# A two-layer diffusion backbone on one core: the second layer's context scores and query preparation put elsewhere in a unit's order

## The chip, the cores and the metric

One Trainium2 chip, of which the program uses one core. The metric is device time in microseconds (us) of one execution. The engines are called PE (TensorE matmul), DVE (VectorE), ACT (ScalarE), POOL (GpSimd) and SP (SyncE, which issues the DMAs).

## The reference

The program runs two layers over 1024 latent tokens with 256 context tokens in front. The first layer (windowed attention and gated mixing) is not touched. The second is multi-head latent attention with 16 heads; what matters of it is this:

```python
def odd_layer(hl, hc, w_in, q_norm, w_qb, kv_norm, w_kvb, w_out, row, col, need_ctx):
    q_a, kv_a, k_pe, gate = jnp.split(hl @ w_in, ODD_SPLITS, axis=-1)
    q = mla_queries(q_a, q_norm, w_qb, row, col)
    k, v = mla_keys_values(kv_a, k_pe, kv_norm, w_kvb, row, col)
    ...
    kc, vc = mla_keys_values(kv_ac, k_pec, kv_norm, w_kvb, None, None)
    o = block_attention(q, jnp.concatenate([k, kc], axis=1), jnp.concatenate([v, vc], axis=1))
    y = (o * jax.nn.silu(gate)) @ w_out
```

So every latent query is scored against 1280 keys (1024 latent, 256 context), goes through a softmax, is multiplied by the values, gated, and projected.

## The kernel before, in words

The attention of the second layer (`layer1_attention`) goes over 64 **units** n. A unit is one head (e = 0 or 1 of the pair hp) and 256 queries (block qg of four); an even unit takes head 0 of a pair and the odd unit after it head 1 with the same 256 queries. The 256 queries stand in two halves j of 128. Eight pairs, four blocks, two heads make 64 units. A unit's work is an exact softmax: scores, maximum, exponential, transposes of the probabilities, products with the values. Products that need more than one pass are split into a high and a low fp32r part.

PSUM has 8 banks: `s0` and `s1` (two each: the 128x1024 scores of the two halves with the latent keys), `sx` (one: both halves' 128x256 scores with the context keys), `tm` (two, taken in turn: transposes and side projections) and `acc` (one: in columns 0 to 255 the products with the values, in columns 256 to 511 the inverse sums).

The order of everything in a unit is written out by hand in `ORDER1` (line 43), and the instructions of PE, ACT, DVE and POOL stand in just that order. The letters, for unit n:

- `S0` to `S3`: latent scores (lines 1228, 1229), one for each 512 columns; `S0 S1` fill `s0`, `S2 S3` fill `s1`. `S4`: the six products of the context's scores into `sx` (lines 1228, 1229, 1231). `K`: the rotary part, four products of 32 rows into `s0` and `s1` (line 1240), which end the latent scores.
- `X0 X1 X2`: maxima on DVE of `s0`, `s1`, `sx` (lines 1251, 1249). `P0 P1`: the two maxima joined (line 1255). `E0 E1`: exponential on ACT of `s0`, `s1`; `E2 E3`: of the two halves of `sx` (line 1266). `E0` must come before the next unit's `S0`, since `s0` is there once.
- `T0` to `T4`: transposes of the probabilities of unit n-1 into `tm`, four of 128x128 each (line 1276), and their copy out: `T0` and `T4` by DVE (line 1285), `T1 T2 T3` by ACT (line 1283). `T0 T1` are half j = 0, `T2 T3` half j = 1, `T4` the context's keys.
- `A0`: half of the products with the values for the pair of units before (line 1294). In an even unit they are keys 0 to 4 of units n-2 and n-1, so they read what `T0` to `T3` of this very unit deliver; in an odd unit keys 5 to 9 of units n-3 and n-2.
- `I`, `U` (odd units): inverse sums, spread by POOL, transposed into `acc` (line 1309). `C` (even units): `gated`, two DVE operations that read `acc` (lines 1318, 1320) and leave it free.
- `D`, `L`: one step each of the side work that prepares the next pair's keys (`prep_pair`) or values (`prep_v`): `D` a projection into `tm`, `L` its copy out. The table `PAIR, VALUES` says in which unit. Keys: ACT copies the high part (line 1153), DVE subtracts the low part (line 1155). Values: ACT copies them (line 1134).
- `B`, `R` (even units): the two steps of `prep_q` for the next 256 queries. `B` loads the rotary part (`pe`, SP, line 1167) and makes six products into a bank (lines 99 to 101). `R`: ACT copies the high part (line 1176), DVE subtracts the low part (line 1178), POOL makes `qc` and `qb` (lines 91, 95).

The table `PAIR, VALUES` gives these kinds of units by their place s in a run of 16: an even unit has a projection of values at s = 6, 10, 12, 14 (in the first three runs), of 512 keys at s = 4, and none otherwise; an odd unit has 512 keys at s = 3, 9, 11, 256 keys at s = 5, 13, and values or none otherwise. Of the 31 even units with a `B` (n = 0 to 60) 12 have values, 4 have 512 keys and 15 have none.

Of the kernel before, what the change touches and what calls it, by code (L numbers as in the profile page):

```python
# [17 lines left out]
D = 1024  # L18
# [21 lines left out]

PAIR, VALUES = (2, 3, 4, 5, 8, 9, 11, 13), (1, 6, 7, 10, 12, 14)
WQ = 'VGG'
ORDER1 = 'S0 S1 T0 T1 I C S2 D S3 K L X0 T2 S4 T3 X2 P0 E0 B X1 P1 E2 R A0 E1 T4 E3 U'.split()
AVS = ((0, 5),), ((5, 10),)
TURNS = 'VAAAV'
KPE = {3: [0], 5: [1]}
# [6 lines left out]
class Kernel:  # L53
# [1103 lines left out]
                self.hi("G", ring[e][0][64:128, c], ring[e][0][0:64, c].bitcast(F32))  # L1157
            yield

    def prep_q(self, hp, qg):  # L1160

        nc = self.nc
        pool = self.qpool[qg % len(self.qpool)]
        cols = slice(qg * self.QG, (qg + 1) * self.QG)
        pe = self.t(self.c1, [P, 2, self.QG], F32, "pe", bufs=1)
        for r in range(0, P, 32):
            nc.sync.dma_start(pe[r:r + 32], self.pe_d[64 * hp:64 * hp + 64, cols].rearrange("(e p) c -> p e c", e=2))
        tp = self.bank()
        w = self.wq[hp]
        for k in range(2):  # L1170
            self.mm3(tp[:, 0:self.QG], *w[k], self.qnh[:, k, cols], self.qnl[:, k, cols], k == 0, k == 1)
        yield
        qa, qb, qc = (self.t(pool, [P, 2, self.QG], F32R, tag, bufs=1) for tag in ("qa", "qb", "qc"))
        src = [tp[64 * e:64 * e + 64, 0:self.QG] for e in range(2)]
        for e in range(2):
            nc.scalar.copy(qa[0:64, e], src[e])  # L1176
        for e in range(2):
            nc.vector.tensor_tensor(qa[64:128, e], src[e], qa[0:64, e].bitcast(F32), op=ALU.subtract)  # L1178
        self.hi("G", qc, pe)
        self.lo("G", qb[96:128], pe[96:128], qc[96:128])  # L1180
        self.hi("G", qb[64:96], pe[64:96])
        self.hi("G", qb[0:64], qa[0:64].bitcast(F32))
        self.pq[(hp, qg)] = [(qa[:, e], qb[:, e], qc[:, e]) for e in range(2)]
        yield

    def layer1_attention(self):
# [24 lines left out]
        banks, peaks, probs, pts, accs, totals, spread = {}, {}, {}, {}, {}, {}, {}  # L1211
# [57 lines left out]
        def turn(n, a):  # L1269
# [14 lines left out]
            else:  # L1284
                nc.vector.tensor_copy(dst, src)  # L1285

        def av(m, k0, k1):
            hp, qg, _ = units[2 * m]
            if k0 == 0:
                accs[m] = self.psum("acc")  # L1290
            for kt in range(k0, k1):
                for e in range(2):
                    vc = ((2 * hp + e) % 4) * 64
                    mm(accs[m][64 * e:64 * e + 64, 0:QG], lhsT=self.v4[hp // 2][:, kt, vc:vc + 64],  # L1294
                       rhs=pts[2 * m + e][:, kt], start=kt == 0, stop=kt == NT - 1)
# [30 lines left out]
        def plan_q(n):  # L1326
            hp, g = n // 8, n % 8 // 2 + 1
            hp, g = (hp + 1, 0) if g == 4 else (hp, g)
            return [self.prep_q(hp, g)] if n % 2 == 0 and hp < 8 else []

        def plan(n):
            s, hp = n % 16, n // 8
# [13 lines left out]
        with self.tc.manual_schedule(engines={E.PE, E.Activation, E.DVE, E.Pool}):  # L1346
            for n in range(N + 3):
                odd = n % 2
                for op in ORDER1:
                    o, a = op[0], int(op[1:] or 0)  # L1350
# [11 lines left out]
                    elif o in "AIU":  # L1362

                        m = (n - 2 - odd) // 2
                        if 0 <= m < N // 2:
                            if o == "A":
                                av(m, *AVS[odd][a])
                            elif odd and o == "I":
                                inverses(m)
                            elif odd:  # L1370
                                inverses_out(m)
                                if n == N + 1:
                                    next(first)
                    elif o == "C":
                        for k in list(accs):
                            if k <= (n - 4) / 2:
                                gated(k)
                    elif o == "B":
                        qs = plan_q(n) if n < N else []
                        for p in qs:  # L1380
                            next(p, None)
                    elif o == "R":
                        for p in qs:
                            next(p, None)
                    elif o == "D":
                        preps = plan(n) if n < N else []
                        for p in preps:
                            next(p, None)
                    elif o == "L":
                        for p in preps:  # L1390
                            next(p, None)
# [214 lines left out]
```

## Time and profile before

| what | value |
|---|---|
| median of 3 runs | 1489.81 us (1490.66, 1489.81, 1485.21) |
| the profiled execution | 1485.86 us, span 1484.1 us |
| busy over the span | PE 1419.7 us (96%), DVE 884.6 (60%), ACT 726.6 (49%), POOL 479.2 (32%) |
| granted TensorE clock over the span | 0.995 |
| the 64 units | about 803 to 1395 us of the span |

The profile was taken of one execution, whose own time is 1485.86 us, 1.76 us more than its span. A PE row of the timeline gives the start and the length of a product, but products overlap: the length (0.28 us for 256 columns) runs until the result is out, while the next one starts after about 0.12 us. What a product costs PE is therefore the distance from its start to the next start, and a wait shows as a distance that is longer than usual.

### The profile page before, as it was taken

How to read it: one execution, taken by the hardware profiler on the slowest of the kernel's cores; microseconds unless marked ns; L12 is line 12 of the kernel's file. 1: busy time of each engine (PE TensorE's matmuls, PEld its weight loads, DVE VectorE, ACT ScalarE, POOL GpSimd, SP SyncE). 2: the span in 40 equal slices, each digit the busy share in tenths (PEclk: the TensorE clock that was granted, in tenths of full speed). 3: DMA queues.
4: the chain of work that ended last, by engine and by line, in shares of the span. 5: the costliest groups of instructions: out<-in, count | busy, mean ns of one | idle time of the engine just before them, and what ended most of it. 6: DMA issues, size and time to landing. Idle time of an engine off the chain costs nothing.

```text
span 1484.1 us, 23403 instructions
## 1 busy us (share of the span) xinstructions
PE 1419.7 (96%) x8849; PEld 1092.8 (74%) x8849; DVE 884.6 (60%) x1692; ACT 726.6 (49%) x1532; POOL 479.2 (32%) x495
## 2 busy tenths in 40 slices
PE   5999999999999699999997999999999999999997
PEld 3766899787666478879886677777777777776786
DVE  5582124346667887543663666776667667776354
ACT  4422310145656644433423666666666666677221
POOL 4343223223556642332183222132213221234100
PEclk9999999999999999999999999999999999999999
DMA  8557501222214446412132110111011111222241
GB/s 332 228 217 272 151 29 30 79 88 79 69 51 157 152 138 192 153 60 79 40 116 94 31 35 29 33 35 35 29 33 34 35 35 45 73 61 90 72 162 72
DMA packets 91465, 138.96 MB, mean 94 GB/s; under 512 B 9088, under 2 KB 67656, under 8 KB 88280
## 3 DMA queue, kind: packets, MB, share of 16 engines
q1 hardware_dynamic: 91208, 137.21, 27.8%
q8 instruction: 69, 1.13, 0.3%
q14 instruction: 44, 0.36, 0.1%
q10 hardware_dynamic: 144, 0.26, 0.0%
HBM read 105.88 MB, written 31.56 MB: 93 GB/s over the span
## 4 chain that ended last, share of the span: by engine, by line
PE 74%; DVE 8%; ACT 6%; issue 5%; DMA 4%; POOL 2%; SPq 0%; POOLq 0%; DVEq 0%; ACTq 0%
PE tm L1276 9%; PE acc L1294 7%; PE s L99 7%; PE s L100 7%; PE s L101 7%; PE b L99 5%; PE b L100 4%; PE b L101 4%; PE s L1228 4%; PE s L1229 3%; PE acc L773 2%; PE tm L99 2%; ACT prob L1266 1%; PE s L1240 1%; DVE kl L1155 1%
## 5 line engine op out<-in xcount | busy, mean ns | idle before, releaser
L1276 PE MATMUL tm<-ident,prob 128*128 128x128 f32 x1280 | 190.6, 279 | 5.1 <-DVE qa L1178 3.4
L1276 PEld LDWEIGHTS tm<-ident,prob 128*128 128x128 f32 x1280 | 141.9, 140 | 59.3 <-issue 22.8
L1283 ACT COPY pt<-tm 128x512 f32<-128x512 f32 x192 | 112.9, 588 | 137.2 <-PE tm L1276 135.6
L1251 DVE TENSOR_REDUCE peak<-s 128x1 f32<-128x1024 f32 x128 | 156.0, 1219 | 29.8 <-PE s L1240 29.1
L1266 ACT ACTIVATE prob<-s,peak 128x1024 f32<-128x1024 f32 x128 | 142.7, 1115 | 37.0 <-DVE peak L1255 34.7
L1294 PE MATMUL acc<-pt,v 128*64 128x256 f32 x1280 | 152.9, 384 | 0.1
L95 POOL TENSOR_TENSOR w_lo<-raw,w_hi 128x512 fp32r<-128x512 f32 (+1 forms) x60 | 74.3, 1251 | 172.2 <-ACT w_hi L87 85.6
L1285 DVE COPY pt<-tm 128x512 f32<-128x512 f32 x128 | 88.4, 690 | 67.2 <-PE tm L1276 65.8
L1294 PEld LDWEIGHTS acc<-pt,v 128*64 128x64 f32 x1280 | 86.4, 136 | 47.3 <-issue 6.1
L1228 PE MATMUL s<-kh,qa 128*128 128x512 f32 x256 | 112.2, 438 | 7.7 <-ACT prob L1266 6.1
L1229 PE MATMUL s<-kl,qb 128*128 128x512 f32 x256 | 101.1, 395 | 0.0
L91 POOL CAST qb<-qa 64x512 fp32r<-64x512 f32 x32 | 19.5, 611 | 190.4 <-ACT qa L1176 190.4
L99 PE MATMUL b<-h,yh 128*128 128x512 f32 x160 | 63.9, 399 | 3.9 <-ACT yh L87 2.9
L99 PE MATMUL s<-h,w_hi 128*128 128x512 f32 x160 | 63.9, 412 | 2.2 <-ACT qk L379 2.2
L100 PE MATMUL s<-h,w_hi 128*128 128x512 f32 x160 | 63.7, 398 | 0.3 <-DVE rs_v L124 0.3
L100 PE MATMUL b<-h,yh 128*128 128x512 f32 x160 | 63.3, 396 | 0.0
L101 PE MATMUL s<-h,w_lo 128*128 128x512 f32 x160 | 63.0, 395 | 0.0
L101 PE MATMUL b<-h,yl 128*128 128x512 f32 x160 | 62.4, 391 | 0.0
L1228 PEld LDWEIGHTS s<-kh,qa 128*128 128x128 f32 x256 | 48.3, 189 | 16.1 <-ACT prob L1266 9.4
L1266 ACT ACTIVATE prob<-sx,peak 128x256 f32<-128x256 f32 x128 | 60.0, 469 | 0.0
L745 DVE TENSOR_TENSOR pt<-pt,tm 128x512 f32<-128x512 f32 x68 | 42.4, 682 | 21.8 <-ACT mb L736 18.9
L751 ACT ACTIVATE pt<-pt 128x512 f32<-128x512 f32 x84 | 47.7, 625 | 13.3 <-DVE pt L745 13.3
(474 smaller groups left out, 3742.8 us busy)
## 6 DMA issues: line engine op xcount, KB each, us to landing
wa<-in_w_ada_dram SPq DMA_DIRECT2D x16, 1024.0 KB, 8.1
x<-in_xs_dram SPq DMA_DIRECT2D x20, 512.0 KB, 6.1
raw<-in_w_dram SPq DMA_DIRECT2D x17, 512.0 KB, 4.4
wa<-in_w_adag_dram SPq DMA_DIRECT2D x8, 1024.0 KB, 6.0
pe<-pe_d SPq DMA_DIRECT2D x128, 64.0 KB, 2.1
raw<-in_w_out_dram SPq DMA_DIRECT2D x10, 512.0 KB, 3.5
yf<-y_d SPq DMA_DIRECT2D x10, 512.0 KB, 6.0
x_d<-x SPq DMA_DIRECT2D x8, 512.0 KB, 4.5
```

The lines of the kernel that those rows point to most:

```text
L95: e.tensor_tensor(lo, src, hi.bitcast(F32), op=ALU.subtract)
L99: mm(out, lhsT=ah, rhs=bh, start=start, stop=False)
L100: mm(out, lhsT=ah, rhs=bl, start=False, stop=False)
L101: mm(out, lhsT=al, rhs=bh, start=False, stop=stop)
L1228: mm(o, lhsT=qa[:, q], rhs=ka[:, k0:k1], start=True, stop=False)
L1229: mm(o, lhsT=qb[:, q], rhs=kb[:, k0:k1], start=False, stop=False)
L1251: nc.vector.reduce_max(m[:, 0, a:a + 1], banks[n, a], axis=AX.X)
L1266: nc.scalar.activation(probs[n][j][:, TL:T] if c else probs[n][j][:, 0:TL], src, AF.Exp, bias=peaks[n][:, 2, j:j + 1], scale=scale, accum_ ...
L1276: nc.tensor.transpose(tp[:, o * P:(o + 1) * P], probs[n][j][:, k * P:(k + 1) * P], self.ident)
L1283: nc.scalar.copy(dst, src)
L1285: nc.vector.tensor_copy(dst, src)
L1294: mm(accs[m][64 * e:64 * e + 64, 0:QG], lhsT=self.v4[hp // 2][:, kt, vc:vc + 64], rhs=pts[2 * m + e][:, kt], start=kt == 0, stop=kt == NT - 1)
```

## The change

The letters of the order are moved: `S4` now stands behind `S3` and in front of `K`, so the six products for the context run on from the latent scores; `X2` stands right behind `X0`; `T2` and `T3` stand next to each other behind `K`. `B` moves up to between `S3` and `S4`, and `R` moves up to behind `L`, in front of `X0`. And `B` no longer takes a bank of `tm`, but the right half of the bank `acc` in which the same unit's `A0` will put its products (for n = 0, where there is none yet, still `tm`).

```diff
-ORDER1 = 'S0 S1 T0 T1 I C S2 D S3 K L X0 T2 S4 T3 X2 P0 E0 B X1 P1 E2 R A0 E1 T4 E3 U'.split()
+ORDER1 = 'S0 S1 T0 T1 I C S2 D S3 B S4 K L R X0 X2 P0 T2 T3 E0 X1 P1 E2 A0 E1 T4 E3 U'.split()
...
-    def prep_q(self, hp, qg):
+    def prep_q(self, hp, qg, bank=None):
...
-        tp = self.bank()
+        tp = (bank or self.bank)()[:, -self.QG:]
         w = self.wq[hp]
         for k in range(2):
-            self.mm3(tp[:, 0:self.QG], *w[k], self.qnh[:, k, cols], self.qnl[:, k, cols], k == 0, k == 1)
+            self.mm3(tp, *w[k], self.qnh[:, k, cols], self.qnl[:, k, cols], k == 0, k == 1)
         yield
...
-        src = [tp[64 * e:64 * e + 64, 0:self.QG] for e in range(2)]
+        src = [tp[64 * e:64 * e + 64] for e in range(2)]
...
+        def acc(m):
+            if m not in accs:
+                accs[m] = self.psum("acc")
+            return accs[m]
+
         def av(m, k0, k1):
             hp, qg, _ = units[2 * m]
             if k0 == 0:
-                accs[m] = self.psum("acc")
+                acc(m)
...
-            return [self.prep_q(hp, g)] if n % 2 == 0 and hp < 8 else []
+            return [self.prep_q(hp, g, (lambda: acc(n // 2 - 1)) if n >= 2 else None)] if n % 2 == 0 and hp < 8 else []
```

Lines behind line 1287 stand seven lines lower in the changed kernel: 1294 is 1301 there, 1318 is 1325.

On PE, in an even unit, from the end of the latent scores (`S3`) to the first product with the values (`A0`). Before:

```order
L1229 MATMUL s_1296_7940<-kl_7092,qb_7797 128x512
L1240 MATMUL s_1291_7917<-kc,qc_7798 128x512 x2
L1240 MATMUL s_1296_7940<-kc,qc_7798 128x512 x2
L1276 MATMUL tm_7960<-ident,prob_7891 128x128 x4
L1228 MATMUL sx_7966<-kh_7091,qa_7796 128x256
L1229 MATMUL sx_7966<-kl_7092,qb_7797 128x256
L1231 MATMUL sx_7966<-kz,qc_7798 128x256
...
L1276 MATMUL tm_7973<-ident,prob_7891 128x128 x4
L99 MATMUL tm_7990<-qnh,w_hi_7545 128x256
L100 MATMUL tm_7990<-qnl,w_hi_7545 128x256
L101 MATMUL tm_7990<-qnh,w_lo_7546 128x256
...
L1294 MATMUL acc_8011<-pt_7831,v_1162_7191 64x256
```

And in the changed kernel:

```order
L1229 MATMUL s_1294_7938<-kl_7092,qb_7773 128x512
L99 MATMUL acc_7955<-qnh,w_hi_7564 128x256
L100 MATMUL acc_7955<-qnl,w_hi_7564 128x256
L101 MATMUL acc_7955<-qnh,w_lo_7565 128x256
...
L1228 MATMUL sx_7962<-kh_7091,qa_7772 128x256
L1229 MATMUL sx_7962<-kl_7092,qb_7773 128x256
L1231 MATMUL sx_7962<-kz,qc_7774 128x256
...
L1240 MATMUL s_1289_7915<-kc,qc_7774 128x512 x2
L1240 MATMUL s_1294_7938<-kc,qc_7774 128x512 x2
L1276 MATMUL tm_7990<-ident,prob_7889 128x128 x4
L1276 MATMUL tm_7996<-ident,prob_7889 128x128 x4
L1301 MATMUL acc_7955<-pt_7829,v_1162_7191 64x256
```

Twelve products (six of `B`, six of `S4`) moved in front of the four rotary ones, and nothing is left between the transposes `T3` and `A0`.

On DVE, in an even unit without a side projection of keys, from the copy of `T0` to the copy of `T4`. Before:

```order
L1285 COPY pt_7922<-tm_7923 128x4x128
L1318 SCALAR_TENSOR_TENSOR gt_7935<-acc_7807,gt_7935 128x256
L1320 TENSOR_TENSOR gt_7935<-acc_7807,gt_7935 128x256
L1251 TENSOR_REDUCE peak_7958<-s_1291_7917 128x1
L1249 TENSOR_REDUCE peak_7958<-sx_7966 128x2
L1255 TENSOR_SCALAR peak_7958<-peak_7958 128x1
L1251 TENSOR_REDUCE peak_7958<-s_1296_7940 128x1
L1255 TENSOR_SCALAR peak_7958<-peak_7958 128x1
L1178 TENSOR_TENSOR qa_8000<-tm_7990,qa_8000 64x256 x2
L1285 COPY pt_7922<-tm_8023 128x512
```

And in the changed kernel:

```order
L1285 COPY pt_7920<-tm_7921 128x4x128
L1325 SCALAR_TENSOR_TENSOR gt_7933<-acc_7748,gt_7933 128x256
L1327 TENSOR_TENSOR gt_7933<-acc_7748,gt_7933 128x256
L1178 TENSOR_TENSOR qa_7975<-acc_7955,qa_7975 64x256 x2
L1251 TENSOR_REDUCE peak_7986<-s_1289_7915 128x1
L1249 TENSOR_REDUCE peak_7986<-sx_7962 128x2
L1255 TENSOR_SCALAR peak_7986<-peak_7986 128x1
L1251 TENSOR_REDUCE peak_7986<-s_1294_7938 128x1
L1255 TENSOR_SCALAR peak_7986<-peak_7986 128x1
L1285 COPY pt_7920<-tm_8020 128x512
```

The queries' two subtractions moved from behind all maxima to in front of them; they read the bank `acc` that the two operations above them have just left.

On ACT, in an even unit without a side projection, from the copy of `T1` to the last exponential. Before:

```order
L1283 COPY pt_10718<-tm_10725 128x4x128
L1283 COPY pt_10718<-tm_10759 128x4x128
L1283 COPY pt_10718<-tm_10772 128x4x128
L1266 ACTIVATE prob_10780,total_10782<-s_1798_10713,peak_10757 128x1024
L1266 ACTIVATE prob_10780,total_10782<-sx_10765,peak_10757 128x256
L1176 CAST qa_10799<-tm_10789 64x256 x2
L1266 ACTIVATE prob_10781,total_10782<-s_1803_10736,peak_10757 128x1024
L1266 ACTIVATE prob_10781,total_10782<-sx_10765,peak_10757 128x256
```

And in the changed kernel:

```order
L1283 COPY pt_10702<-tm_10709 128x4x128
L1176 CAST qa_10760<-acc_10734 64x256 x2
L1283 COPY pt_10702<-tm_10775 128x4x128
L1283 COPY pt_10702<-tm_10781 128x4x128
L1266 ACTIVATE prob_10787,total_10789<-s_1782_10697,peak_10771 128x1024
L1266 ACTIVATE prob_10787,total_10789<-sx_10741,peak_10771 128x256
L1266 ACTIVATE prob_10788,total_10789<-s_1787_10720,peak_10771 128x1024
L1266 ACTIVATE prob_10788,total_10789<-sx_10741,peak_10771 128x256
```

The queries' two copies moved from between the exponentials to in front of the copies of `T2` and `T3`.

## Rows read from the trace of the kernel before

**Rows 1.** Busy time by stretch, the 64 units: us, PE, PEld, DVE, ACT, POOL, clock, DMA, GB/s.
```profile
803.00:1395.00 592.00, 579.01 (x4165) 427.06 (x4164) 400.89 (x706) 384.82 (x848) 156.50 (x221) 1.00 0.14 42
```

**Rows 2.** What PE waited for, 800 to 1400 us: total us, times, longest.
```profile
PE s L1228 <- ACT prob L1266: 6.1, 14, 1.9
PE tm L1276 <- DVE qa L1178: 3.4, 5, 0.8
```

**Rows 3.** Timeline of PE, one even unit without a side projection: start, us, instruction.
```profile
1110.23 0.48 PE L1228 MATMUL s<-kh,qa 128*128 128x512 f32 x1
...
1112.84 0.39 PE L1229 MATMUL s<-kl,qb 128*128 128x512 f32 x1
1113.15 0.50 PE L1240 MATMUL s<-kc,qc 32*128 32x512 f32 x4
1113.59 0.66 PE L1276 MATMUL tm<-ident,prob 128*128 128x128 f32 x4
1114.00 0.37 PE L1228 MATMUL sx<-kh,qa 128*128 128x256 f32 x1
...
1114.81 0.60 PE L1276 MATMUL tm<-ident,prob 128*128 128x128 f32 x4
1115.16 0.36 PE L99 MATMUL tm<-qnh,w_hi 128*128 128x256 f32 x1
1115.36 0.28 PE L100 MATMUL tm<-qnl,w_hi 128*128 128x256 f32 x1
...
1115.83 0.28 PE L101 MATMUL tm<-qnh,w_lo 128*128 128x256 f32 x1
1116.04 2.38 PE L1294 MATMUL acc<-pt,v 128*64 128x256 f32 x20
...
1118.76 0.48 PE L1228 MATMUL s<-kh,qa 128*128 128x512 f32 x1
```

**Rows 4.** Timeline of DVE and of ACT, the same unit: gated's last operation, T2's copy.
```profile
1112.95 0.42 DVE L1320 TENSOR_TENSOR gt<-acc,gt 128x256 f32<-128x256 f32 x1
...
1114.28 0.59 ACT L1283 COPY pt<-tm 128x512 f32<-128x512 f32 x1 [1.36 <-PE tm L1276]
```

**Rows 5.** Timeline of ACT and of DVE, copies and subtractions of the queries.
```profile
903.48 0.73 ACT L1176 CAST qa<-tm 64x256 fp32r<-64x256 f32 x2
...
904.30 0.86 DVE L1178 TENSOR_TENSOR qa<-tm,qa 64x256 fp32r<-64x256 f32 x2 [1.11 <-ACT qa L1176]
```

**Rows 6.** Timeline of PE, DVE, ACT, an odd unit with a projection of 512 keys.
```profile
904.62 0.48 PE L1228 MATMUL s<-kh,qa 128*128 128x512 f32 x1
...
910.14 0.66 PE L1276 MATMUL tm<-ident,prob 128*128 128x128 f32 x4
...
914.08 0.50 PE L1228 MATMUL s<-kh,qa 128*128 128x512 f32 x1 [0.17 <-ACT prob L1266]
...
909.23 1.39 DVE L1155 TENSOR_TENSOR kl<-tm,kh 64x512 fp32r<-64x512 f32 x2 [1.99 <-ACT kh L1153]
910.66 1.23 DVE L1251 TENSOR_REDUCE peak<-s 128x1 f32<-128x1024 f32 x1
...
912.82 1.12 ACT L1266 ACTIVATE prob<-s,peak 128x1024 f32<-128x1024 f32 x1 [1.40 <-DVE peak L1255]
```

**Rows 7.** Timeline of PE, first score product of other units.
```profile
923.49 0.48 PE L1228 MATMUL s<-kh,qa 128*128 128x512 f32 x1
...
932.02 0.48 PE L1228 MATMUL s<-kh,qa 128*128 128x512 f32 x1
...
983.98 0.50 PE L1228 MATMUL s<-kh,qa 128*128 128x512 f32 x1 [0.17 <-ACT prob L1266]
...
993.69 0.48 PE L1228 MATMUL s<-kh,qa 128*128 128x512 f32 x1
...
1003.23 0.48 PE L1228 MATMUL s<-kh,qa 128*128 128x512 f32 x1
```

**Rows 8.** DMA issues, the queries' rotary part: count, KB each, us to landing.
```profile
pe<-pe_d SPq DMA_DIRECT2D x128, 64.0 KB, 2.1
```

## The prediction, on record before the changed kernel was run

> **What bounds the kernel now.** First the busy time of the stretch that the change touches: in the 592 us of the 64 units PE is busy 579 us at a granted clock of 1.00, while DVE has 401 and ACT 385 [rows 1]. So PE bounds these units, its clock is at the higher level already, and a new order can gain only waits. Second the waits of PE there: 6.1 us for the exponential and 3.4 us, five times, for the queries' subtraction [rows 2]. Little is to be had. Third one unit's timeline, for what each step costs and how far ahead the other engines are. The unit at 1110.23 takes 8.53 us to the next one's first product [rows 3], with no gap. A score product of 512 columns costs about 0.235 us (the last starts at 1112.84, and `K` at 1113.15, 0.08 us later than that gives). A product of 256 columns costs 0.117 us in a run (1115.36 to 1115.83 is four), and 0.20 us when it comes first after other work [rows 3].
>
> The wait that can hurt is the one for `E0`: there is one `s0`, so a unit's first product waits for the exponential of the unit before. In the odd unit with keys the whole chain can be read [rows 6]: DVE's subtraction of the keys ends at 909.23 + 1.39 = 910.62; the first maximum starts at 910.66; `E0` at 912.82; the next unit's first product at 914.08, and it waited. So **from the first maximum to the next unit's first product is 914.08 - 910.66 = 3.42 us**, whatever PE does. A unit is as long as the longer of two things: PE's own sum, or the start of its first maximum plus 3.42 us. (Handing over from one engine to another takes 0.04 us: 910.62 to 910.66. I use it throughout.)
>
> **The change, part by part.** Times are from a unit's first product.
>
> *PE's own sum* hardly changes: the same products. Between `S3` and `K` there are now `B` (six products, 0.70 us) and `S4` (0.70 us), so `K` and the first maximum behind it come 0.70 us later in an odd unit and 1.40 us later in an even one. Not having `S4` between `T2` and `T3` could save at most the slow first product, 0.20 - 0.12 = 0.08 us a unit, 5 us in all; but the four transposes in front of `S4` cost 0.41 us (1113.59 to 1114.00) and those in front of `B` 0.35 [rows 3]; the early start of the product behind them is part of the same 0.08, so I take 0 and keep 5 us as the other end. The Trainium skill, "TensorEngine Tiling (Array Packing)", section Tiling Modes, has a rule that speaks against a gain here: PE drains when the tiling mode changes, not when only the tile does. Transposes and scores both show 128\*128, so by that rule mixing them costs nothing; only `K` (32\*128) and `A0` (128\*64) are other modes, and both kernels enter each once a unit. By the rule the sum is 0 here, by the row's outer bound -5 us.
>
> *The queries in front of the maxima (even units).* `R` now stands before the first maximum on DVE. From the last product of `B`: it takes 0.28 us until its result is out [rows 3], 0.04 to hand over, ACT copies for 0.73, DVE starts 0.09 later and subtracts for 0.86 [rows 5], 0.03 to the first maximum. That is 2.03 us from the start of `B`'s last product, and 3.42 more to the next unit. On DVE the maxima, on ACT the copies of `T2` and `T3`, stand behind it.
>
> *`B` waits for `acc`.* The bank is free when `gated` has ended: 1112.95 + 0.42 = 1113.37, that is 3.14 us into the unit [rows 3, 4], and `B` can start at 3.19.
>
> - Even, no side projection: PE would reach `B` at (1112.84 - 1110.23) + 0.235 = 2.84, so it waits 0.35. First product at 3.19, the second 0.20 later, the last at 3.86; first maximum at 5.89; next unit at 9.31 instead of 8.53: **+0.78**. Thirteen units (n = 8 to 60): +10.1. The unit n = 2 has nothing to gate: `B` at 2.84, last product at 3.43, next unit at 8.88: +0.35.
> - Even, with values: the projection adds 923.49 - 914.08 - 8.53 = 0.88 us before `B` [rows 3, 6, 7], which then starts at 3.72 and finds the bank free. Last product at 4.31, first maximum at 6.34, next unit at 9.76 instead of 9.41: **+0.35**. Twelve units: +4.2.
> - Even, with 512 keys: the keys' subtraction ends 6.00 us into a unit [rows 6] and now stands in front of the queries', which run to 6.89; first maximum 6.92, next unit 10.34 instead of 993.69 - 983.98 = 9.71 [rows 7]: **+0.63**. Four units: +2.5.
>
> *`A0` loses its cover (even units).* It reads the copy of `T2`, which ends 1114.28 + 0.59 - 1113.59 = 1.28 us after `T2` begins [rows 3, 4]. Before, `S4`, `T3` and `B` lay between. Now only `T3` does, and PE arrives after 1.02 us (0.41 + 0.08 for `T2`, and 0.35 + 0.88 - 0.70 for `T3` up to `A0` without the six products [rows 3]). So it waits 0.31 us. PE's own sum in an even unit without projection then is 3.19 + 0.79 (`B`) + 0.70 (`S4`) + 0.08 + 0.44 (`K`) + 1.33 + 2.72 (`A0` to the next unit [rows 3]) = 9.25, just under the 9.31 of the chain; with values 9.69 under 9.76. The two waits lie beside each other: if either were gone, the other would keep nearly all of the loss.
>
> *A wait that goes.* The five waits for the queries' subtraction [rows 2] are for a bank of `tm`, four of them in the odd unit with 256 keys behind an even one with 512. That unit takes 1003.23 - 993.69 = 9.54 us; its like without the wait takes 932.02 - 923.49 = 8.53 [rows 7]. `B` no longer holds a bank of `tm`: **-1.01**, four units: -4.0.
>
> *Odd units with 512 keys.* Without `B` in the rotation, `T3` gets the bank from which the keys are subtracted, and waits until 6.00 + 0.05; now it started at 910.14, 5.52 into the unit [rows 6]. From there 0.53 to `A0`, 2.72 on, and 0.22 for the two transposes of `U` (0.11 each, as four take 0.41): 9.52 against 9.46 now, +0.06. Ten units: +0.6. Other odd units have their first maximum about 4.2 us in (`K` at 2.84 + 0.78, 0.50 until done [rows 3]), so the chain ends at 7.6, under their 8.05 (8.53 - 0.70 + 0.22): nothing.
>
> *The rest.* `S4` waits for the last exponential of the unit before. If `E0` ends as the unit begins, three are left: 1.12 us for 1024 columns [rows 6] and at most half of that for each of 256, so 2.24 us; `S4` comes at 2.84 or later: nothing. On SP the four loads of `pe` keep their place behind the store of the unit's gated block; they land after 2.1 us [rows 8] and POOL needs them a unit later. POOL's four operations only start earlier; its load is 157 of 592 us [rows 1].
>
> **Sum:** 10.1 + 0.35 + 4.2 + 2.5 - 4.0 + 0.6 = +13.8 us on the profiled 1485.86, so 1499.7. The profiled execution lies 4 us under the median, and with the three runs shown there are two near 1485.5 and two near 1490; against their mean of 1487.9 the changed kernel's runs should lie around **1502 us**.
>
> **Bounds of the unknown.** Not seen before: how `A0` behaves when only one head's probabilities are there. If its two heads no longer run side by side in the first step, up to 0.2 us more in each of 29 units, of which the 0.06 us under the chain cover some: +5. The chain's 3.42 us contains no wait that I know of; 0.1 us either way in it is 3 us. The mixing, if it does save 0.08, saves it only in odd units, where no chain stands: -2.6. With 2.5 us for which of the two levels a median falls on: 1494 to 1511.
>
> **Rivals.**
>
> *The chain and the copy stay covered, and the kernel is faster.* The place is the way from `B` to the next unit's first maximum. It decides at 0.35 us: if copies and subtractions of the queries end that much earlier than I add up (for instance because both run per head side by side, ACT on one while DVE takes the other), and `A0` begins with the head that is there, only the removed waits count: -4.0 and up to -5 for the mixing, so 1487.9 - 9 = 1479. For it: the waits are real [rows 2]. Against: DVE started only behind both copies [rows 5], and two mechanisms must fail together. Chance 0.07.
>
> *Only the bank costs.* If chain and copy are covered but `B` waits for `gated`: 13 x 0.43 (0.35 and a slow first product) + 0.6 - 4.0 = +2.2, so 1490, which no measurement here can tell from no change (0.5%, 7.4 us). With part of the other losses it would be anything up to 1497. Chance 0.13.
>
> *That the change does not do what it says:* the order in the program shows the moves on all three engines, so I give it nothing of its own.
>
> **Chances.** My case 0.80, all slower by over 0.5%; the bank alone or a partial loss 0.13, within 0.5%; covered 0.07, faster. The range 1494 to 1511 is the forecast's own, and reaches into the second case.
>
> **What would show it.** Right: even units without a projection last 9.3 us, with values 9.75, with 512 keys 10.3, and the first score product after them waits for the exponential; DVE starts the first maximum right behind the queries' subtraction; odd units with 256 keys behind even ones with 512 last 8.5; `B` starts at 3.2 us in a unit without projection, and PE's busy share in the stretch falls. Wrong: even units at 8.5 and 9.4 us; a first maximum that starts behind `K` and not behind the subtraction; or waits of odd units that I held to be free.

## The result, and the profile after

The changed kernel takes **1510.52 us** (median of 5 runs, 1508.88 to 1510.78), the kernel before beside it 1488.83 us (median of 5): a ratio of **1.0145, 95% interval 1.0131 to 1.0159**. It is slower by 1.45%, within the range given and near its upper end; the forecast was 1502.

Its page has these totals:

```profile
span 1509.0 us, 23393 instructions
...
PE 1437.3 (95%) x8849; PEld 1120.1 (74%) x8849; DVE 880.6 (58%) x1692; ACT 721.2 (48%) x1532; POOL 477.9 (32%) x495
```

The busy time by stretch, for the 64 units [rows 1], and then for the first units alone:

```profile
803.00:1395.00 592.00, 569.21 (x4017) 435.87 (x4016) 389.12 (x691) 369.46 (x827) 149.87 (x215) 0.99 0.14 41
...
817.60:820.90 3.30, 3.30 (x12) 2.81 (x13) 0.36 (x2) 1.95 (x6) 0.00 (x0) 0.52 0.00 0
...
826.60:831.00 4.40, 4.38 (x16) 3.82 (x17) 2.02 (x6) 2.56 (x7) 0.71 (x2) 0.61 0.02 4
```

In the same 592 us PE is busy 10 us less than before, and 148 of its products have not been reached yet. The other two rows are for later: granted clocks of 0.52 and 0.61.

What PE waited for, 800 to 1400 us, in place of [rows 2]:

```profile
PE s L1228 <- ACT prob L1266: 8.6, 9, 4.0
PE tm L1276 <- DVE kl L1155: 6.0, 10, 0.6
PE acc L99 <- DVE gt L1327: 1.8, 6, 0.3
PE acc L99 <- DVE w_hi L89: 1.8, 6, 0.3
```

The five waits for the queries' subtraction on a bank of `tm` have gone. New are the waits of `B` (line 99) for `acc` and ten waits of `T3` for the keys' subtraction. (The `w_hi` row is the same wait put down to another operation of DVE: in the experiment that moves `gated` alone both rows vanish.) One of the ten, PE and then DVE:

```profile
1068.57 0.63 PE L1276 MATMUL tm<-ident,prob 128*128 128x128 f32 x4 [0.59 <-DVE kl L1155]
...
1067.03 1.39 DVE L1155 TENSOR_TENSOR kl<-tm,kh 64x512 fp32r<-64x512 f32 x2 [1.99 <-ACT kh L1153]
```

Timeline of PE, of an even unit without a side projection (n = 32; the one in [rows 3] is n = 34):

```profile
1108.18 0.48 PE L1228 MATMUL s<-kh,qa 128*128 128x512 f32 x1
...
1110.76 0.39 PE L1229 MATMUL s<-kl,qb 128*128 128x512 f32 x1
1111.46 0.36 PE L99 MATMUL acc<-qnh,w_hi 128*128 128x256 f32 x1 [0.31 <-DVE gt L1327]
...
1112.12 0.28 PE L101 MATMUL acc<-qnh,w_lo 128*128 128x256 f32 x1
...
1113.03 0.51 PE L1240 MATMUL s<-kc,qc 32*128 32x512 f32 x4
1113.47 1.09 PE L1276 MATMUL tm<-ident,prob 128*128 128x128 f32 x8
1114.49 2.68 PE L1301 MATMUL acc<-pt,v 128*64 128x256 f32 x20
1117.10 0.66 PE L1276 MATMUL tm<-ident,prob 128*128 128x128 f32 x4
1117.64 0.50 PE L1228 MATMUL s<-kh,qa 128*128 128x512 f32 x1
```

And DVE, then ACT, in that unit:

```profile
1110.89 0.42 DVE L1327 TENSOR_TENSOR gt<-acc,gt 128x256 f32<-128x256 f32 x1
1113.32 0.86 DVE L1178 TENSOR_TENSOR qa<-acc,qa 64x256 fp32r<-64x256 f32 x2 [2.01 <-ACT qa L1176]
1114.21 1.23 DVE L1251 TENSOR_REDUCE peak<-s 128x1 f32<-128x1024 f32 x1
...
1112.49 0.74 ACT L1176 CAST qa<-acc 64x256 fp32r<-64x256 f32 x2 [1.64 <-PE acc L101]
1114.16 1.07 ACT L1283 COPY pt<-tm 128x512 f32<-128x512 f32 x2 [0.93 <-PE tm L1276]
1116.38 1.11 ACT L1266 ACTIVATE prob<-s,peak 128x1024 f32<-128x1024 f32 x1 [1.15 <-DVE peak L1255]
```

The whole chain of the prediction can be read off. `gated` ends at 1111.31, `B` starts 0.15 us later, ACT copies, DVE subtracts until 1114.18, the first maximum starts at 1114.21, and the next unit's first product at 1117.64, that is 3.43 us behind it. The unit lasts 9.46 us where it lasted 8.53.

Sorting all units by kind shows where the time went. Each number in the first five columns is the median distance from a unit's first score product to the next unit's (13, 12, 4, 4 and 10 units); the sixth is units 0 to 2 together; the seventh is the change from the first product of unit 0 to that of unit 63, against before. The last is the ratio of the whole times with its interval. The rows of the experiments are discussed below.

| kernel | even, none | even, values | even, 512 keys | odd behind it | odd, 512 keys | n = 0 to 2 | change | ratio |
|---|---|---|---|---|---|---|---|---|
| before | 8.53 | 9.39 | 9.70 | 9.55 | 9.48 | 22.2 | | |
| **the change** | 9.46 | 9.78 | 10.36 | 8.55 | 9.67 | 27.5 | +23.6 | 1.0145 [1.0131, 1.0159] |
| scores alone | 8.99 | 9.87 | 10.15 | 9.08 | 9.67 | 25.0 | +16.6 | 1.0088 [1.0073, 1.0103] |
| queries alone | 9.46 | 9.79 | 10.38 | 8.55 | 9.49 | 25.3 | +20.5 | 1.0132 [1.0117, 1.0147] |
| no subtraction | 9.35 | 9.63 | 9.64 | 8.53 | 9.64 | 26.7 | +15.2 | 1.0070 [1.0055, 1.0085] |
| gated first | 8.91 | 9.78 | 10.36 | 8.54 | 9.67 | 27.1 | +16.2 | 1.0096 [1.0079, 1.0113] |
| first units as before | 9.45 | 9.77 | 10.36 | 8.54 | 9.67 | 23.2 | +19.2 | 1.0117 [1.0100, 1.0133] |
| both waits removed | 8.51 | 9.37 | 9.48 | 8.55 | 9.46 | 25.1 | -2.9 | 0.9974 [0.9965, 0.9984] |
| T2 before K | 8.52 | 9.81 | 12.31 | 11.46 | 12.31 | 27.2 | +78.8 | 1.0552 [1.0532, 1.0572] |
| keys' low part later | 8.53 | 9.39 | 10.50 | 8.72 | 9.07 | 22.2 | -3.8 | 0.9968 [0.9955, 0.9980] |

Of the +23.6 us the 13 even units without a projection carry 12.5, the 12 with values 4.7, the 4 with keys 2.4, the 10 odd units with 512 keys 2.0, units 0 to 2 5.3 and the last two before unit 63 0.7; the odd units behind even ones with keys give back 4.0. (Of the 12.5, 0.35 is one unit, n = 50, which took 9.81 us; in the run "first units as before" no unit of its kind does.)

### The profile page after: what moved, and what is told of

It is laid out like the page before. It is cut to its first block, busy times and chain, and to the rows that moved or that the text cites. A ratio compares the mean times of both kernels' runs of the same rounds, so it can differ in the third digit from the quotient of the medians.

```text
span 1509.0 us, 23393 instructions
## 1 busy us (share of the span) xinstructions
PE 1437.3 (95%) x8849; PEld 1120.1 (74%) x8849; DVE 880.6 (58%) x1692; ACT 721.2 (48%) x1532; POOL 477.9 (32%) x495
## 4 chain that ended last, share of the span: by engine, by line
PE 72%; DVE 9%; ACT 6%; issue 5%; DMA 5%; POOL 2%; SPq 0%; POOLq 0%; DVEq 0%; ACTq 0%
PE acc L1301 9%; PE tm L1276 9%; PE s L99 6%; PE s L100 6%; PE s L101 5%; PE b L99 5%; PE b L100 4%; PE b L101 4%; PE s L1228 4%; PE s L1229 3%; PE acc L773 2%; PE s L1240 1%; PE tm L99 1%; DMA yf<-y_d 1%; ACT kh L1153 1%
## 5 line engine op out<-in xcount | busy, mean ns | idle before, releaser
L1276 PE MATMUL tm<-ident,prob 128*128 128x128 f32 x1280 | 183.1, 280 | 8.2 <-DVE kl L1155 6.0
L1301 PE MATMUL acc<-pt,v 128*64 128x256 f32 x1280 | 160.6, 384 | 0.8 <-DVE qa L1178 0.7
L1283 ACT COPY pt<-tm 128x512 f32<-128x512 f32 x192 | 108.0, 588 | 103.9 <-PE tm L1276 102.8
L1301 PEld LDWEIGHTS acc<-pt,v 128*64 128x64 f32 x1280 | 103.7, 136 | 40.0 <-issue 10.3
L1228 PE MATMUL s<-kh,qa 128*128 128x512 f32 x256 | 113.3, 443 | 10.1 <-ACT prob L1266 8.6
L1310 POOL COPY spread<-total 128x256 f32<-128x256 f32 x32 | 12.7, 397 | 168.5 <-DVE total L1309 168.5
L1178 DVE TENSOR_TENSOR qa<-acc,qa 64x256 fp32r<-64x256 f32 x60 | 25.4, 423 | 53.8 <-ACT qa L1176 48.9
```

The source lines that it names most:

```text
L1228: mm(o, lhsT=qa[:, q], rhs=ka[:, k0:k1], start=True, stop=False)
L1276: nc.tensor.transpose(tp[:, o * P:(o + 1) * P], probs[n][j][:, k * P:(k + 1) * P], self.ident)
L1283: nc.scalar.copy(dst, src)
```

## The experiments

**The two halves apart.** First the run of five scores alone, as an edit of the kernel before: `B` and `R` stay where they were, in `tm`.

```diff
-ORDER1 = '... S3 K L X0 T2 S4 T3 X2 P0 E0 B X1 P1 E2 R A0 E1 T4 E3 U'.split()
+ORDER1 = '... S3 S4 K L X0 X2 P0 T2 T3 E0 B X1 P1 E2 R A0 E1 T4 E3 U'.split()
```

> Half of the change: context's score S4 stands with the other scores, but the queries stay in a tile of the ring of two banks and stand behind the units' last scores, as before. If the queries' new place is what costs (the copy and the subtractions stand ahead of the two maxima on DVE, and the side projection B waits for the accumulator), the even units go back to what they had before: 8.5 us without a side projection, 9.4 with values, 9.7 with 512 keys; only the odd units with 512 keys keep what the scores' run gives them there, T3's wait for the keys' subtraction (9.6 to 9.7 instead of 9.46). Whole time 1487 to 1492 us. If instead the late rotary part and the run of five scores carry a share of the loss, the even units stay at 8.8 us or more and the time is 1495 us or more.

Measured: 1502.65 us (4 runs), ratio 1.0088. The theory missed: every even unit lost 0.45 to 0.48 us, with the queries where they always were. The timeline of ACT and of PE in one of them says how:

```profile
1107.96 1.08 ACT L1283 COPY pt<-tm 128x512 f32<-128x512 f32 x2 [2.07 <-PE tm L1276]
...
1107.27 1.09 PE L1276 MATMUL tm<-ident,prob 128*128 128x128 f32 x8
1108.60 0.39 PE L99 MATMUL tm<-qnh,w_hi 128*128 128x256 f32 x1 [0.24 <-ACT pt L1283]
```

`T2` and `T3` take the two banks of `tm` one right after the other, and `B`, next in turn, waits until ACT has copied `T2` out. Before, `S4` lay between `T2` and `T3` and covered that copy. So this half is not free by itself, and the forecast's rival (a late rotary part) is not shown by it either: there is a third cause. The halves don't add up (16.6 and 20.5 alone, 23.6 together), because with `B` in `acc` this wait is gone.

Then the queries alone, as an edit of the changed kernel, with `S4` between `T2` and `T3`:

```diff
-ORDER1 = '... S3 B S4 K L R X0 X2 P0 T2 T3 E0 X1 P1 E2 A0 E1 T4 E3 U'.split()
+ORDER1 = '... S3 B K L R X0 T2 S4 T3 X2 P0 E0 X1 P1 E2 A0 E1 T4 E3 U'.split()
```

> The other half: the queries in the accumulator's bank and in front of the products, but S4 between T2 and T3 with the rotary part as before. If the queries' place carries the loss, the even units stay at 9.4 to 9.5 us (no side projection), 9.7 to 9.8 (values) and 10.3 (512 keys), the first three units keep their 5 us of loss, and only the odd units with 512 keys return to 9.46: 1506 to 1509 us. If the run of scores shares the loss, the even units without a side projection lie at 9.0 us or less and the time is about 1500 us.

Measured: 1509.06 us, ratio 1.0132. Even units 9.46, 9.79 and 10.38, odd ones with 512 keys 9.49, all as expected; only units 0 to 2 lost 3.1 us and not 5. Here `A0` is covered again (it takes 2.31 us up to `T4`, as before, and not 2.61) and the unit lasts just as long, since the chain holds it. The wait of the next unit's first product, in total, times and longest, has become the main one:

```profile
PE s L1228 <- ACT prob L1266: 14.8, 44, 3.8
```

**The chain and the bank, one at a time.** The changed kernel without the queries' subtraction (the low half is a copy of the high half):

```diff
-        for e in range(2):
-            nc.vector.tensor_tensor(qa[64:128, e], src[e], qa[0:64, e].bitcast(F32), op=ALU.subtract)
+        self.hi("G", qa[64:128], qa[0:64].bitcast(F32))
```

> The changed kernel without DVE's two subtractions that make the queries' low half; POOL writes a copy of the high half in their place, so the output is not the reference's. DVE has 1.2 us less to do between the copy of the queries and the first maximum, nothing else moves. If the even unit's period is the chain from the accumulator over R and the maxima to the next unit's first product, it shortens until the next wait takes over: B still waits for the accumulator and A0 still waits for T2's copy, so 9.2 to 9.35 us without a side projection, 9.6 with values, 9.6 with 512 keys, together 6 to 7 us less than the changed kernel, about 1504. If that chain alone makes the loss, the even units fall to 8.8 to 8.9 us and 9.4, about 1490 to 1494.

Measured: 1500.07 us, ratio 1.0070. The even units came out as expected (9.35, 9.63, 9.64) and gave 6.6 us; units 0 to 2 and the others gave 1.8 more. That makes 8.4 of the 10.4 us by which the medians differ. The two profiled executions, from which the table comes, differ by 9.4 only, and in them unit 0 starts 1.0 us earlier without the subtraction, behind work that no edit touches: over the ten traces it starts anywhere from 807.7 to 811.5 us. From the last product of `B` to the first maximum it is now 1.55 us (1106.82 to 1108.37) instead of 2.09 (1112.12 to 1114.21), and the maximum waits for `K`. Yet the unit gains only 0.11. The timelines of DVE and PE, for the unit's end:

```profile
1108.37 1.23 DVE L1250 TENSOR_REDUCE peak<-s 128x1 f32<-128x1024 f32 x1 [2.35 <-PE s L1239]
...
1106.82 0.28 PE L101 MATMUL acc<-qnh,w_lo 128*128 128x256 f32 x1
...
1109.22 2.68 PE L1300 MATMUL acc<-pt,v 128*64 128x256 f32 x20
1111.83 0.66 PE L1275 MATMUL tm<-ident,prob 128*128 128x128 f32 x4
1112.24 0.48 PE L1227 MATMUL s<-kh,qa 128*128 128x512 f32 x1
```

The next unit's first product follows `T4` by 0.41 us, the time four transposes cost [rows 3], so it waits for nothing: PE's own path with its two waits is 9.35 us, just under the chain's 9.46. In the changed kernel the same distance was 0.54 us (1117.10 to 1117.64).

The changed kernel with `gated` as the first thing DVE does in a unit:

```diff
-ORDER1 = 'S0 S1 T0 T1 I C S2 D S3 B S4 K ...'.split()
+ORDER1 = 'C S0 S1 T0 T1 I S2 D S3 B S4 K ...'.split()
```

> The changed kernel with the gate's product C issued first in a unit on DVE, ahead of the scores' and the transposes' steps, so that the accumulator is free when B wants it. If the wait of B for the accumulator is on the path of the even units without a side projection, each of those 13 loses the 0.3 to 0.45 us of that wait: 9.0 to 9.1 us instead of 9.46, the units with values and keys as in the changed kernel, about 1505 us. If the chain over R and the maxima sets the period by itself and the wait only fills time that would be idle later, nothing changes: 9.4 to 9.5, 1510 us.

Measured: 1504.30 us, ratio 1.0096. The even units without a projection fell from 9.46 to 8.91, further than the 9.0 to 9.1 expected, and no other kind of unit moved. `gated` now ends before `B` is reached, and `B` follows the scores without a gap:

```profile
1107.49 0.48 PE L1228 MATMUL s<-kh,qa 128*128 128x512 f32 x1
...
1110.07 0.39 PE L1229 MATMUL s<-kl,qb 128*128 128x512 f32 x1
1110.30 0.28 PE L99 MATMUL acc<-qnh,w_hi 128*128 128x256 f32 x1
...
1115.88 0.66 PE L1276 MATMUL tm<-ident,prob 128*128 128x128 f32 x4
1116.41 0.50 PE L1228 MATMUL s<-kh,qa 128*128 128x512 f32 x1
```

So of the 0.93 us of these units 0.55 hang on the bank and 0.38 on what stands behind `B`. The first product still comes 0.53 us behind `T4`, later than the 0.41 of four transposes: the chain holds the unit, only from an earlier `B`. PE's own path here would be 0.12 us shorter, about 8.8 by this estimate, so without the chain `A0`'s wait would still keep some 0.3 us.

Both together: queries alone (so `S4` stands between `T2` and `T3`, and `A0`'s wait is gone as well), with `gated` first and without the subtraction.

```diff
-ORDER1 = 'S0 S1 T0 T1 I C S2 D S3 B S4 K L R X0 X2 P0 T2 T3 E0 X1 P1 E2 A0 E1 T4 E3 U'.split()
+ORDER1 = 'C S0 S1 T0 T1 I S2 D S3 B K L R X0 T2 S4 T3 X2 P0 E0 X1 P1 E2 A0 E1 T4 E3 U'.split()
...
-        for e in range(2):
-            nc.vector.tensor_tensor(qa[64:128, e], src[e], qa[0:64, e].bitcast(F32), op=ALU.subtract)
+        self.hi("G", qa[64:128], qa[0:64].bitcast(F32))
```

> Queries in front of the products as in the change, S4 between T2 and T3 as before, the gate's product first in a unit and no subtractions for the queries (a copy of the high half stands for the low half, so the output is not the reference's): both waits that the theory blames are gone. If they make the whole loss of the even units, those lie at 8.5 to 8.6 us without a side projection and 9.4 with values, and the time at 1483 to 1492 us. If the queries' products in front of the second layer's products cost by themselves (a third cause), the even units stay over 8.9 us and the time over 1496.

Measured: 1484.75 us (9 runs), ratio 0.9974. The even units are back at 8.51 and 9.37, and those with keys at 9.48 are better than before: nothing else in the queries' new place costs them time. Units 0 to 2, though, still lose 2.9 us (25.1). The part of the change that was right shows as well, in the odd units behind them, 8.55 instead of 9.55.

**The start.** The changed kernel with the order (`FIRST1` is the `ORDER1` of before) and the bank of before for units 0 to 2:

```diff
-            return [self.prep_q(hp, g, (lambda: acc(n // 2 - 1)) if n >= 2 else None)] if n % 2 == 0 and hp < 8 else []
+            return [self.prep_q(hp, g, (lambda: acc(n // 2 - 1)) if n >= 4 else None)] if n % 2 == 0 and hp < 8 else []
...
-                for op in ORDER1:
+                for op in (FIRST1 if n < 3 else ORDER1):
```

> The changed kernel, but the first three units run in the order of before, with the queries in the ring's bank until the fourth. If the 5 us that units 0 to 2 lose come from R standing ahead of the first maxima there (TensorE waits 4 us for the first probabilities, and its granted clock is lower behind that), they take 22 us together instead of 27.5 and the whole falls by about 5 us, to 1505. If the loss there comes from elsewhere (the stage before the units, the clock alone), it stays at 1509 to 1511.

Measured: 1505.92 us, ratio 1.0117. Units 0 to 2 take 23.2 us instead of 27.5, and no other kind of unit moved by more than 0.02 us. What they lost is to be seen in the timelines of PE, of the kernel before (first row), of the changed kernel (the next four) and of this run, with the clock of a stretch of this run behind it:

```profile
813.73 0.50 PE L1228 MATMUL s<-kh,qa 128*128 128x512 f32 x1 [1.92 <-ACT prob L1266]
...
817.60 0.80 PE L1228 MATMUL s<-kh,qa 128*128 128x512 f32 x1 [3.98 <-ACT prob L1266]
818.19 0.63 PE L1229 MATMUL s<-kl,qb 128*128 128x512 f32 x1
818.62 0.63 PE L1228 MATMUL s<-kh,qa 128*128 128x512 f32 x1
...
826.62 0.51 PE L1228 MATMUL s<-kh,qa 128*128 128x512 f32 x1 [1.48 <-ACT prob L1266]
...
816.16 0.50 PE L1229 MATMUL s<-kh,qa 128*128 128x512 f32 x1 [1.91 <-ACT prob L1267]
...
816.16:820.20 4.04, 4.04 (x15) 3.43 (x16) 1.54 (x3) 3.42 (x10) 0.61 (x1) 0.58 0.00 0
```

In unit 0 nothing of an earlier unit is there to transpose or to multiply, so after its scores PE has nothing to do until `E0`: 3.98 us, where before it was 1.92. Most of the 2.06 us between is not `R`, as I had expected, but the twelve products of `B` and `S4`. They used to run behind `K`, beside the first maximum; now they stand in front of `K` and leave PE idle behind it (1.4 us at 0.117 each [rows 3]). Without the subtraction the wait is still 3.46 us, and in the run of scores alone, with `R` in its old place, 2.63. Unit 0 lasts 7.93 us instead of 6.03.

The other 3.4 us are lost in units 1 and 2. Behind the wait products of 512 columns are 0.43 us apart (818.19 to 818.62) instead of 0.235, and the granted clock of that stretch is 0.52, close to the lower of the two levels (1.2 GHz); between 826.6 and 831 it fell once more. The Trainium skill, "TensorE: Matmul & The Clock Gate", section HAM oscillation, says that a long enough wait of PE lets its clock be throttled, so that the work behind it starts cold. The trace agrees here, but the length of the wait alone does not tell: behind the 1.92 us of before the clock stayed at 1.00, and behind the 1.91 us of this run it fell (0.58 from 816.16 to 820.20). The first three units are those of before here, unit 0 lasts 6.04 us, and the 1.0 us that they still take longer lies behind that fall: so a part of the 5.3 us need not be the order's.

**A mend of the scores' run that was not one.** To test the reading of the first experiment, `T2` moves ahead of `K`:

```diff
-ORDER1 = '... S3 S4 K L X0 X2 P0 T2 T3 E0 B X1 P1 E2 R A0 E1 T4 E3 U'.split()
+ORDER1 = '... S3 S4 T2 K L X0 X2 P0 T3 E0 B X1 P1 E2 R A0 E1 T4 E3 U'.split()
```

> The run of scores alone, as in the experiment that missed, with one step moved: the transposes T2 stand ahead of the rotary part K instead of behind it, so that K lies between T2 and T3; the rotary part and the first maximum come later still. In that experiment B's bank in the ring of two is the one that ACT is still copying T2 from, since nothing lies between T2 and T3 any more. If that wait is the 0.46 us that each even unit lost there, K's 0.43 us cover it: the even units go from 9.0 to 8.55 to 8.65 us without a side projection and from 9.87 to 9.4 to 9.5 with values, the time to 1490 to 1493 us. If the late rotary part costs it (the first maximum and the probabilities too late for the next unit), it stays or grows: 9.0 us or more, 1502 us or more.

Measured: 1569.20 us, ratio 1.0552. In the units for which it was meant the reading holds: even ones without a projection are at 8.52, and `B` follows `T3` without a wait (0.41 us behind its start, in the first two rows). But an order is an order for every engine, and I had moved `T2`'s copy ahead of `L` on ACT as well: with values the even units stayed at 9.81, and with keys everything got far worse. PE in an even unit, then ACT, DVE and PE in an odd one with 512 keys:

```profile
1145.85 0.66 PE L1276 MATMUL tm<-ident,prob 128*128 128x128 f32 x4
1146.26 0.37 PE L99 MATMUL tm<-qnh,w_hi 128*128 128x256 f32 x1
...
1173.98 0.59 ACT L1283 COPY pt<-tm 128x512 f32<-128x512 f32 x1 [2.18 <-PE tm L1276]
1174.46 1.18 ACT L1153 CAST kh<-tm 64x512 fp32r<-64x512 f32 x2
...
1175.68 1.39 DVE L1155 TENSOR_TENSOR kl<-tm,kh 64x512 fp32r<-64x512 f32 x2 [4.16 <-ACT kh L1153]
1177.10 1.23 DVE L1251 TENSOR_REDUCE peak<-s 128x1 f32<-128x1024 f32 x1
...
1180.52 0.50 PE L1228 MATMUL s<-kh,qa 128*128 128x512 f32 x1 [2.13 <-ACT prob L1266]
```

ACT stands idle 2.18 us for the transposes while the keys' projection lies ready, copies `T2` first, and then the chain runs its course: subtraction, first maximum, and 3.42 us later (1177.10 to 1180.52) the next unit. That is the prediction's chain again, at its predicted price, in another unit. For the late rotary part the even units without a projection are clean: `K` starts 4.07 us into them, against 2.92 before and 3.61 in the run of scores alone, and they are as short as ever, so there it costs nothing. Where `L` moved with it, the run does not decide.

**The chain used for a gain.** If a subtraction in front of the first maximum costs what it lasts, the kernel before has one too: the keys' in its ten odd units with 512 keys [rows 6]. In the kernel before, this step alone is put off until behind `E0`:

```diff
-ORDER1 = '... X2 P0 E0 B X1 ...'.split()
+ORDER1 = '... X2 P0 E0 M B X1 ...'.split()
...
-            for e in range(2):
-                nc.vector.tensor_tensor(ring[e][1][0:64, c], src[e], ring[e][0][0:64, c].bitcast(F32), op=ALU.subtract)
+            def low(c=c, src=src):
+                for e in range(2):
+                    nc.vector.tensor_tensor(ring[e][1][0:64, c], src[e], ring[e][0][0:64, c].bitcast(F32), op=ALU.subtract)
+            if self.later is None:
+                low()
+            else:
+                self.later.append(low)
...
+                    elif o == "M":
+                        while self.later:
+                            self.later.pop(0)()
```

> The kernel before, with one step moved: DVE's subtractions for the keys' low half stand behind the first maximum and its probabilities E0 instead of right behind the keys' copy. In the odd units with 512 keys they stand on the chain to the first maximum as the queries' subtractions do in the changed kernel. If that chain sets those units' period, ten of them go from 9.46 to about 8.9 us and the wait at the next transposes in some units goes too: 1478 to 1483 us, 0.4 to 0.7% below the kernel before. If the keys' subtractions are covered, nothing changes: 1486 to 1490; if the tile's bank, held longer, makes the next transposes wait, 1490 or more.

Measured: **1483.48 us** (9 runs) against 1487.90 (19 runs), ratio 0.9968, 0.9955 to 0.9980: 0.3% faster than the kernel before, just above the range expected. DVE, then PE, in one of the ten:

```profile
891.18 1.23 DVE L1257 TENSOR_REDUCE peak<-s 128x1 f32<-128x1024 f32 x1 [1.69 <-PE s L1246]
...
893.33 1.38 DVE L1157 TENSOR_TENSOR kl<-tm,kh 64x512 fp32r<-64x512 f32 x2
...
886.86 0.49 PE L1234 MATMUL s<-kh,qa 128*128 128x512 f32 x1
...
895.79 0.38 PE L1315 MATMUL acc<-ident,spread 128*128 128x128 f32 x2
895.93 0.48 PE L1234 MATMUL s<-kh,qa 128*128 128x512 f32 x1
...
990.97 0.39 PE L99 MATMUL tm<-qnh,w_hi 128*128 128x256 f32 x1 [0.68 <-ACT pt L1289]
```

The unit is 9.07 us long instead of 9.48 (8.9 was expected) and PE no longer waits at its end; 0.41 us of 1.39 is all there was, since PE's own path comes next. Ten units gave 4.0 us. The even units with keys lost 0.8 each, because the bank is held longer and `B` has to take the one of `T3` and waits for its copy (0.68 us, last row), and the odd units behind them won 0.8 each, as there the wait for the queries' subtraction is gone; the three other odd units with 256 keys lost 0.2 each.

## Why the prediction was right, and where not

- **The chain** was right in place and price. 3.42 us from the first maximum to the next unit were read as 3.43; values 9.76 predicted, 9.78 measured; 512 keys 10.34, 10.36 measured; the odd units behind them 8.53, 8.55. Leaving out the subtraction, freeing the bank early and putting `S4` back between `T2` and `T3` brought the even units back together (8.51, 9.37), and none of the three did alone (9.35, 8.91, 9.46).
- **"If either were gone, the other would keep nearly all of the loss"** held for the two waits it speaks of, the chain's and `A0`'s: without the subtraction 0.11 of 0.93 us came back, because PE's own path (predicted 9.25, measured 9.35) binds next; with `A0` covered again nothing came back (9.46). `A0`'s wait was priced right, too: 0.31 predicted, and from `A0` to the next unit 3.02 us (1109.22 to 1112.24) against 2.72 [rows 3]. What I did not say is that `B`'s wait stands at the head of both paths, so freeing the bank alone did give 0.55.
- **Handing over "0.04 us, I use it throughout"** is the term that was too small. I took it from DVE to DVE (its own order). From DVE's last access of a bank to PE's first product in it 0.15 us passed, both for `B` (1111.31 to 1111.46) and for `T3`, which started at 1068.57 behind a subtraction that ended at 1068.42. [rows 6] had a hand-over to PE already: `E0` ends at 912.82 + 1.12 = 913.94, and the product that waits for it starts at 914.08. With 0.06 more from `B`'s last product to the first maximum (2.09 instead of 2.03) the 13 units came to 9.46 instead of 9.31: 12.5 us, not 10.1, with the 0.35 of n = 50. `T3`'s term was +0.06 a unit and is +0.2: 2.0 us in ten units, not 0.6.
- **"The unit n = 2: +0.35", and nothing for n = 0 and 1** is the step that failed outright: 5.3 us. I priced the chain in units where it lies beside PE's work of two earlier units. In unit 0 there is none, so all that stands in front of the maxima is lost: 1.9 us, of which the twelve moved products make 1.4. The other 3.4 came in units 1 and 2, where the clock fell twice. The first-units run gave 4.3 of the 5.3 back; the last 1.0 came with a fall of the clock in units that are those of before.
- **The run of scores saves nothing**: odd units without a projection last 8.03 us, 8.02 before. By the rule of the Trainium skill ("TensorEngine Tiling (Array Packing)", Tiling Modes) cited in the prediction it was to be 0, and the trace agrees; the other end, -5 us, is out.
- **Sum**: 13.8 predicted, 23.6 measured in the units: of the 9.8 between, 5.0 come from the start, 2.4 and 1.4 from the two terms with the hand-over, 0.5 from values and 0.7 from unit 61, one of the last, for which I had put nothing. The median rose by 21.7 us; the two profiled executions are 24.9 apart, 2.0 of them ahead of unit 0, so the sum is that of one pair.
- **The range** held in part by luck: it left 5 us for `A0`, 3 for the chain's price and 2.5 for the median's level. Neither of the first two was needed: `A0` cost what the sum has for it, and the chain's 3.42 held. What filled the room was the start and the hand-over.

## What to carry to other kernels

Where a hand-written order feeds several engines, list for a step that is moved what it comes in front of on *each* of them: here 0.86 us of subtractions on an engine that is busy 58% of the time made, together with one wait for a bank and one lost cover, most of a loss of 1.45%, since they came to stand between the scores and the maximum on which the next unit waits. A bank that is "free anyway" has a time at which it becomes free: compare that with the time at which the new user arrives, in every kind of unit, and add the hand-over. And price the first units by themselves: there only the unit's own products cover its chain, and those that are moved in front of it cover nothing.

## What was not expected of the hardware

- PE resumed 0.15 us after DVE's last access to the bank it waited for, in two different places, where DVE went on to its own next instruction after 0.03 to 0.04 us.
- One idle stretch of 3.98 us was followed by 3.3 us at a granted clock of 0.52, and by a second stretch at the lower level (0.61 from 826.6 to 831 us) behind a wait of only 1.48 us; the kernel before, with a wait of 1.92 us at the same place, stayed at 1.00, while the run with the first units as before, with 1.91 us, had 0.58 over the next 4 us. What decides between them no run here shows.
